# ConvGLU up projection: GpSimd takes the low part of the value half's weights, and the later convolutions accumulate in a PSUM bank

## The chip, the cores and the metric

The kernel runs on one core of a Trainium2 chip, in one launch. Its time is the device time of an execution in microseconds (us). The engines are named as the profile names them: PE (TensorE matmul), PEld (its weight load), DVE (VectorE), ACT (ScalarE), POOL (GpSimd) and SP (SyncE, which issues most DMAs).

## What is computed

One layer of a hybrid backbone: a token mixer, then a ConvGLU channel mixer, on 512 tokens (8 rows of 64) of width 1024. The change is in the channel mixer, whose reference is:

```python
def _conv_ffn(h, rows, w_up, conv_w, conv_b, w_down):      # w_up (1024, 2 x 2816), w_down (2816, 1024)
    a, val = _split(h @ w_up, (D_FF, D_FF))
    img = a.reshape(bsz, rows, length // rows, D_FF)
    a = lax.conv_general_dilated(img, conv_w[:, :, None, :], (1, 1), 'SAME', ...,
                                 feature_group_count=D_FF) + conv_b      # 3 x 3, each channel by itself
    return (jax.nn.gelu(a.reshape(bsz, length, D_FF), approximate=False) * val) @ w_down
```

## The kernel before

**Products.** All operands are fp32. A matrix is split into a high part rounded to fp32r and a low part, the rest; a product is then three matmuls per piece (high x high, high x low, low x high). The up projection goes through the 2816 channels in 22 steps `f` of 128 channels. A step has two products, one for the image half (the columns that are convolved) and one for the value half. A product is 24 matmuls (8 pieces of the inner dimension, 3 each) into one PSUM bank of the pool `pm` (four banks, tiles `mm`). Below, product j = 2f is the image half of step f, and j = 2f + 1 its value half; there are 44. The other four banks are the pool `pg` (tiles `gl`), which the up projection leaves alone and the down projection uses as accumulators.

**Weights.** For each product a tile `raw` (128 x 1024, 512 KB) is loaded by SP (L148) into one of four buffers; ACT rounds it into `wh` (L138), and DVE subtracts, `wl = raw - wh` (L139). `wh` and `wl` have five buffers each, so ACT can round a tile as soon as PE has ended the product five before it.

**A step's elementwise work** is `conv_part(f, pa, pv)`. ACT copies the image bank `pa` into the SBUF tile `ca` (L1422) and writes bias plus centre tap into the SBUF tile `cacc` (L1424). DVE adds the eight other taps, each a scalar_tensor_tensor `cacc = ca * w + cacc` (L1430). ACT applies Gelu (L1431), DVE multiplies by the value bank `pv` (L1432). After each odd step DVE forms four sums over token halves (L1413 to L1416), which a Strassen-like down projection needs.

**Down projection.** It needs the gated channels as its left operand and `ffn_w_down` as weights. Weight tiles come into the same four `raw` buffers (L1457) and, with an addition on the way, into `b22` tiles (load by SP, L1453; accumulating DMA by POOL, L1454). DVE adds two halves of a `raw` tile (L1485), forms `t2` (L1489) and the low parts (L1475, L354); ACT rounds (L1474, L353). PE accumulates (L1532) in eight banks: four `gl` (the products `p1` and `p5`, two each) and four `mm` (`p7`, `p6`).

**Order.** Each engine works off its own queue in order. A scheduler places the instructions of the traced program in these queues, so code written in one place can stand among that of the next step, and preparation of the down projection stands among the last steps of the up projection.

Of the kernel before, what the change touches and what calls it, by code (L numbers as in the profile page):

```python
# [8 lines left out]
F32 = mybir.dt.float32  # L9
# [3 lines left out]
AF = mybir.ActivationFunctionType  # L13
ALU = mybir.AluOpType
AX = mybir.AxisListType

P = 128
# [3 lines left out]
KT = 8  # L21
NH = 4
FF = 2816
FT = 22
GW = 64
# [8 lines left out]
def backbone_kernel(  # L34
# [7 lines left out]
    V, A, G, T = nc.vector, nc.scalar, nc.gpsimd, nc.tensor  # L42
# [11 lines left out]
    def nm(s):  # L54
        cnt[0] += 1
        return f"{s}_{cnt[0]}"

    def heap(shape, dt=F32, s="h"):
        return hp.tile(shape, dt, tag="h", name=nm(s))

    def late(shape, dt=F32, s="l"):
        return lp.tile(shape, dt, tag="l", name=nm(s))
# [4 lines left out]
    def mm():  # L67
        return pm.tile([P, 512], F32, tag="mm", name=nm("mm"))

    def gl():  # L70
        return pg.tile([P, 512], F32, tag="gl", name=nm("gl"))

    def const(shape, s, dt=F32):
        return cp.tile(shape, dt, tag=s, name=s)
# [57 lines left out]
    def raw_tile(kn, n):  # L132
        return wp.tile([P, kn, n], F32, tag="raw", name=nm("raw"), bufs=4)

    def split_new(raw, kn, n):
        wh = wp.tile([P, kn, n], F32R, tag="wh", name=nm("wh"))
        wl = wp.tile([P, kn, n], F32R, tag="wl", name=nm("wl"))
        A.copy(wh, raw)  # L138
        V.tensor_tensor(wl, raw, wh.bitcast(F32), op=ALU.subtract)  # L139
        return wh, wl  # L140

    def w_cols(w, c0, n=P, k0=0, kn=KT, scaled=False):
        ap = w[k0 * P:(k0 + kn) * P, c0:c0 + n].rearrange("(k p) c -> p k c", p=P)
        held = []

        def load():
            held.append(raw_tile(kn, n))
            dma(held[0], ap)  # L148

        def split():  # L150
            if not scaled:
                return split_new(held.pop(), kn, n)
            raw = held.pop()
            wh = wp.tile([P, kn, n], F32R, tag="wh", name=nm("wh"))
            wl = wp.tile([P, kn, n], F32R, tag="wl", name=nm("wl"))
            for kk in range(kn):
                g_ = gng[:, k0 + kk:k0 + kk + 1]
                A.mul(wh[:, kk, :], raw[:, kk, :], g_)
                V.scalar_tensor_tensor(wl[:, kk, :], raw[:, kk, :], g_, wh[:, kk, :].bitcast(F32), op0=ALU.mult,
                                       op1=ALU.subtract)  # L160
            return wh, wl

        loads.append((len(specs), load))
        specs.append(split)

    def w_wide(w, scaled=False):
        for hf in range(2):
            for k in range(KT // 2):
                w_cols(w, hf * 512, 512, 2 * k, 2, scaled)

    def w_strassen(w, c0):
# [32 lines left out]
        def split_raw(name, j):  # L204
            return lambda: split_new(raws.pop((name, j)), 2, 512)
# [12 lines left out]
        def split_b11(j):  # L218
            def split():
                raws["b11k", j] = raws["b11", j]  # L220
                return split_new(raws.pop(("b11", j)), 2, 512)
            return split
# [11 lines left out]
    for h in range(1, NH):  # L234
        if h > 1:
            w_cols(wi, O_V + h * 256, 256, 0, 4)
            w_cols(wi, O_V + h * 256, 256, 4, 4)
        for hh in ((1, 2), (3,), ())[h - 1]:
            w_cols(wi, O_K + hh * P)
            w_cols(wi, O_Q + hh * P)  # L240
# [10 lines left out]
    w_wide(w_o[0])  # L251
    for f in range(FT):
        w_cols(ffn_w_up[0], f * P)
        w_cols(ffn_w_up[0], FF + f * P)

    splits = {}
    pos = [0, 0, 0]
# [13 lines left out]
    def weights(lead=1, ahead=AHEAD):  # L271
        i = pos[2]
        pos[2] += 1
        stream_split(i + 1 + lead)
        stream_load(i + 1 + ahead)
        return splits.pop(i)
# [50 lines left out]
    for d in range(2):  # L327
        raw = late([96, 512], s="w2r")
# [393 lines left out]
    for k in range(KT):  # L722
# [10 lines left out]
        n = 0  # L733
# [286 lines left out]
    for t in range(2):  # L1020
        ps = mm()
        for k in range(KT):
            wh, wl = fv[k // 2][1:]
# [128 lines left out]
    ccol = const([P, 220], "ccol")  # L1152
# [24 lines left out]
    for j in range(KT):  # L1177
        w = weights()
# [225 lines left out]
    gact, s12, s4 = [], [], []  # L1404
    flat = lambda z: z.rearrange("p r w -> p (r w)")

    def token_sums(p):

        e, o = flat(gact[2 * p]), flat(gact[2 * p + 1])
        s = late([P, 2, 256], s="s12")  # L1410
        if p % 2 == 0:
            s4.append(late([P, 2, 256], s="s4"))
        V.tensor_tensor(s[:, 0, :], o[:, 256:], e[:, 256:], op=ALU.subtract)  # L1413
        V.tensor_tensor(s[:, 1, :], s[:, 0, :], e[:, :256], op=ALU.add)
        V.tensor_tensor(e[:, 256:], e[:, :256], e[:, 256:], op=ALU.subtract)
        V.tensor_tensor(s4[-1][:, p % 2, :], s[:, 1, :], o[:, :256], op=ALU.subtract)  # L1416
        s12.append(s)

    def conv_part(f, pa, pv):
        wcol = lambda tap: ccol[:, tap * FT + f:tap * FT + f + 1]  # L1420
        a_ = heap([P, 8, GW], s="ca")
        A.copy(a_, pa)  # L1422
        acc = heap([P, 8, GW], s="cacc")
        A.activation(acc, pa, AF.Identity, bias=ccol[:, 198 + f:199 + f], scale=wcol(4))  # L1424
        for tap in (0, 1, 2, 3, 5, 6, 7, 8):
            dy, dx = tap // 3 - 1, tap % 3 - 1
            r0, r1 = max(0, -dy), 8 - max(0, dy)
            c0, c1 = max(0, -dx), GW - max(0, dx)
            o = acc[:, r0:r1, c0:c1]
            V.scalar_tensor_tensor(o, a_[:, r0 + dy:r1 + dy, c0 + dx:c1 + dx], wcol(tap), o, op0=ALU.mult, op1=ALU.add)  # L1430
        A.activation(acc, acc, AF.Gelu)  # L1431
        V.tensor_tensor(acc, acc, pv.rearrange("p (r w) -> p r w", w=GW), op=ALU.mult)  # L1432
        gact.append(acc)
        if f % 2:
            token_sums(f // 2)

# [3 lines left out]
    for i in range(4):  # L1440
        prod_cm(pss[i][:, 256:], ws[i], h2, 256, 256)
    conv_part(0, pss[0], pss[1])
    conv_part(1, pss[2], pss[3])

    NP = FT // 2
# [106 lines left out]
    for f in range(2, FT):  # L1552
        pa = mm()
        prod_cm(pa, weights(), h2)
        pv = mm()
        prod_cm(pv, weights(), h2)
        if f == FT - 2:
            d_load(4)
        if f == FT - 1:
            d_load(7)  # L1560
            for i in range(LEAD):
                prep(i)
        conv_part(f, pa, pv)
# [163 lines left out]
```

## Time and profile before

| | |
|---|---|
| time, median of 3 runs | 930.37 us |
| the profiled execution | 931.34 us, of which the span of the trace is 929.6 us |
| PE busy | 907.7 us, 98% of the span |
| DVE busy | 755.2 us, 81% |
| ACT busy | 447.8 us, 48% |
| POOL busy | 52.8 us, 6% |

The span is the time from the first to the last instruction of the trace; 1.74 us of the execution lie around it. The trace gives for each instruction its engine, its line in the code and its start; for idle time it names what ended it.

### The profile page before, as it was taken

Reading aid. Unit: us, or ns where it says so; the run is one execution under the profiler, and the core shown is the slowest. Engines: PE = TensorE matmul, PEld = TensorE weight load, DVE = VectorE, ACT = ScalarE, POOL = GpSimd, SP = SyncE. Lnnn points to the kernel's source line nnn. Section 1 sums busy time; section 2 is a strip of 40 time slices with the busy share of each in tenths; the row PEclk is TensorE's granted clock in tenths of the full one; section 3 lists DMA queues with packets and bytes.
Section 4 is the critical chain, followed back from the end, with each engine's and each line's share of the span. In section 5 each row is a group of like instructions: output and inputs, shape, how many; then the busy total and the mean of one; then the engine's idle time right before and its main releaser. Section 6 shows DMA issues by size and latency. Waiting matters only on the chain.

```text
span 929.6 us, 12825 instructions
## 1 busy us (share of the span) xinstructions
PE 907.7 (98%) x4695; PEld 761.1 (82%) x4695; DVE 755.2 (81%) x1349; ACT 447.8 (48%) x787; POOL 52.8 (6%) x80
## 2 busy tenths in 40 slices
PE   6999999999999999999999999999999999999996
PEld 5776898988878888888878888988888888878885
DVE  5567758689689978866789987798888888999797
ACT  5136546457443337755652334543333333366574
POOL 3000000000000011112100000000000000132000
PEclk9999999999999999999999999999999999999998
DMA  9940411132077384885649642333333333399432
GB/s 275 336 130 24 136 47 46 46 96 64 23 228 231 112 227 90 230 212 144 187 127 340 228 142 78 102 94 95 109 92 91 93 109 110 85 251 246 127 101 91
DMA packets 123547, 130.06 MB, mean 140 GB/s; under 512 B 6953, under 2 KB 84085, under 8 KB 123485
## 3 DMA queue, kind: packets, MB, share of 16 engines
q1 hardware_dynamic: 114781, 115.75, 40.2%
q0 software_dynamic: 6976, 12.28, 8.0%
q10 hardware_dynamic: 1728, 1.22, 0.4%
q8 instruction: 37, 0.61, 0.3%
q14 instruction: 25, 0.20, 0.1%
HBM read 127.13 MB, written 2.10 MB: 139 GB/s over the span
## 4 chain that ended last, share of the span: by engine, by line
PE 82%; DVE 10%; ACT 2%; DMA 2%; issue 2%; SPq 1%; ACTq 0%; DVEq 0%
PE mm L361 27%; PE mm L387 13%; PE gl L434 7%; PE gl L1532 6%; PE mm L434 5%; PE mm L1532 4%; PE gl L387 4%; PE gl L876 3%; PE mm L380 3%; DVE cacc L1430 2%; PE mm L372 1%; PE mm L666 1%; PE mm L980 1%; DVE bc L844 1%; DVE wl L139 1%
## 5 line engine op out<-in xcount | busy, mean ns | idle before, releaser
L138 ACT CAST wh<-raw 128x1024 fp32r<-128x1024 f32 x110 | 115.4, 1052 | 148.8 <-PE mm L361 99.8
L139 DVE TENSOR_TENSOR wl<-raw,wh 128x1024 fp32r<-128x1024 f32 x110 | 133.9, 1220 | 43.7 <-ACT wh L138 43.3
L361 PE MATMUL mm<-h2h,wh 128*128 128x512 f32 (+1 forms) x352 | 133.5, 379 | 0.0
L361 PE MATMUL mm<-h2l,wh 128*128 128x512 f32 (+1 forms) x352 | 133.5, 379 | 0.0
L361 PE MATMUL mm<-h2h,wl 128*128 128x512 f32 (+1 forms) x352 | 133.5, 379 | 0.0
L1430 DVE SCALAR_TENSOR_TENSOR cacc<-ca,ccol,cacc 128x441 f32<-128x441 f32 (+2 forms) x176 | 121.7, 695 | 4.1
L361 PEld LDWEIGHTS mm<-h2h,wh 128*128 128x128 f32 x352 | 66.2, 188 | 12.5
L361 PEld LDWEIGHTS mm<-h2l,wh 128*128 128x128 f32 x352 | 66.2, 188 | 12.4
L361 PEld LDWEIGHTS mm<-h2h,wl 128*128 128x128 f32 x352 | 66.2, 188 | 12.4
L1125 DVE SCALAR_TENSOR_TENSOR acc<-wa,cs,acc 128x512 f32<-128x512 f32 x64 | 45.1, 744 | 2.1 <-DMA wa<-in_w_ada_dram 2.1
L387 PE MATMUL mm<-wh,trh 128*128 128x512 f32 x112 | 44.4, 397 | 0.0
L387 PE MATMUL mm<-wh,trl 128*128 128x512 f32 x112 | 44.0, 392 | 0.0
L387 PE MATMUL mm<-wl,trh 128*128 128x512 f32 x112 | 43.7, 390 | 0.0
L1431 ACT ACTIVATE cacc<-cacc 128x512 f32<-128x512 f32 x22 | 13.9, 633 | 58.5 <-DVE cacc L1430 58.5
L361 PE MATMUL mm<-hxh,wh 128*128 128x512 f32 x104 | 41.7, 401 | 0.0
L361 PE MATMUL mm<-hxh,wl 128*128 128x512 f32 x104 | 41.0, 394 | 0.0
L361 PE MATMUL mm<-hxl,wh 128*128 128x512 f32 x104 | 40.7, 391 | 0.0
L1474 ACT CAST wh<-raw 128x1024 fp32r<-128x1024 f32 x22 | 23.0, 1052 | 20.5 <-PE mm L1532 6.1
L1454 POOL DMA_DIRECT2D b<-in_ffn_w_down_dram x11 | 9.4, 878 | 370.5 <-DMA b<-in_ffn_w_down_dram 356.8
L1475 DVE TENSOR_TENSOR wl<-raw,wh 128x1024 fp32r<-128x1024 f32 x22 | 26.8, 1219 | 4.4 <-ACT wh L1474 4.3
L186 POOL DMA_DIRECT2D tt<-in_w_in_dram x24 | 20.9, 1135 | 166.2 <-DVE hu L1207 77.5
L434 PE MATMUL mm<-wh,hxh 128*128 128x512 f32 x72 | 28.0, 389 | 0.0
(489 smaller groups left out, 2323.5 us busy)
## 6 DMA issues: line engine op xcount, KB each, us to landing
raw<-in_w_in_dram SPq DMA_DIRECT2D x54, 512.0 KB
wa<-in_w_ada_dram SPq DMA_DIRECT2D x96, 256.0 KB
raw<-in_ffn_w_up_dram SPq DMA_DIRECT2D x44, 512.0 KB
raw<-in_ffn_w_down_dram SPq DMA_DIRECT2D x22, 512.0 KB
tt<-in_w_in_dram POOLq DMA_DIRECT2D x24, 256.0 KB, 7.7
raw<-in_w_br_a_dram SPq DMA_DIRECT2D x8, 512.0 KB
raw<-in_w_br_b_dram SPq DMA_DIRECT2D x8, 512.0 KB
raw<-in_w_o_dram SPq DMA_DIRECT2D x8, 512.0 KB
```

Of the source, the lines that this page charges most:

```text
L138: A.copy(wh, raw)
L139: V.tensor_tensor(wl, raw, wh.bitcast(F32), op=ALU.subtract)
L361: T.matmul(ps, a[:, k, :], b[:, c0:c0 + n], start=(k == 0 and i == 0), stop=(k == KT - 1 and i == 2))
L380: T.matmul(ps, a[:, t * P:(t + 1) * P], b[:, k % 4, :], start=(k == 0 and i == 0), stop=(k == KT - 1 and i == 2))
L387: T.matmul(ps, a, b[:, k % 2, :], start=(k == 0 and i == 0), stop=(k == KT - 1 and i == 2))
L434: T.matmul(ps[t], a, b[:, kk, :], start=(first and i == 0), stop=(j == 1 and kk == 1 and i == 2), skip_group_check=again)
L876: T.matmul(ps, p_, q_, start=(start and z == 0), stop=(stop and z == 2))
L1125: V.scalar_tensor_tensor(acc[j], w_, cs[:, k, 0:1], acc[j], op0=ALU.mult, op1=ALU.add)
L1430: V.scalar_tensor_tensor(o, a_[:, r0 + dy:r1 + dy, c0 + dx:c1 + dx], wcol(tap), o, op0=ALU.mult, op1=ALU.add)
L1474: A.copy(wh, raw)
L1475: V.tensor_tensor(wl, raw, wh.bitcast(F32), op=ALU.subtract)
L1532: T.matmul(ps, a[:, t * P:(t + 1) * P], w[b][:, j, c0:c0 + n], start=(first and i == 0), stop=(last and i == 2), skip_group_check=again)
```

## The change

For steps f >= 3 the subtraction that makes `wl` of the value half is issued on GpSimd instead of VectorE. For steps f >= 11 the convolution's accumulator is a `gl` PSUM bank: ACT writes bias and centre tap there, DVE accumulates the taps there, and Gelu reads it and writes the SBUF tile `cacc`, which the rest of the kernel uses as before. Lines below L1423 are one higher than before in the changed kernel.

```diff
-    def split_new(raw, kn, n):
+    def split_new(raw, kn, n, eng=None):
         ...
         A.copy(wh, raw)
-        V.tensor_tensor(wl, raw, wh.bitcast(F32), op=ALU.subtract)
+        (eng or V).tensor_tensor(wl, raw, wh.bitcast(F32), op=ALU.subtract)
         return wh, wl
...
     for f in range(FT):
         w_cols(ffn_w_up[0], f * P)
-        w_cols(ffn_w_up[0], FF + f * P)
+        w_cols(ffn_w_up[0], FF + f * P, eng=G if f >= 3 else None)
...
         A.copy(a_, pa)
-        acc = heap([P, 8, GW], s="cacc")
-        A.activation(acc, pa, AF.Identity, bias=ccol[:, 198 + f:199 + f], scale=wcol(4))
+        g_ = heap([P, 8, GW], s="cacc")
+        acc = gl().rearrange("p (r w) -> p r w", w=GW) if f >= FT // 2 else g_
+        A.activation(acc, pa.rearrange("p (r w) -> p r w", w=GW), AF.Identity, bias=..., scale=wcol(4))
         for tap in (0, 1, 2, 3, 5, 6, 7, 8):
             ...
             V.scalar_tensor_tensor(o, a_[...], wcol(tap), o, op0=ALU.mult, op1=ALU.add)
-        A.activation(acc, acc, AF.Gelu)
-        V.tensor_tensor(acc, acc, pv.rearrange("p (r w) -> p r w", w=GW), op=ALU.mult)
-        gact.append(acc)
+        A.activation(g_, acc, AF.Gelu)
+        V.tensor_tensor(g_, g_, pv.rearrange("p (r w) -> p r w", w=GW), op=ALU.mult)
+        gact.append(g_)
```

The change also moves instructions at three places. On PE, at the start of the down projection, `gl_7770` to `gl_7773` are the four accumulators before; the rows are the fifth to the twelfth matmul of the down projection.

```order
L1532 MATMUL gl_7771<-wl_7716,eh_7720 128x512
L1532 MATMUL gl_7771<-wh_7715,el_7721 128x512
L1532 MATMUL gl_7772<-wh_7715,sh_7724 128x512
L1532 MATMUL gl_7772<-wl_7716,sh_7724 128x512
L1532 MATMUL gl_7772<-wh_7715,sl_7725 128x512
L1532 MATMUL gl_7773<-wh_7715,sh_7724 128x512
L1532 MATMUL gl_7773<-wl_7716,sh_7724 128x512
L1532 MATMUL gl_7773<-wh_7715,sl_7725 128x512
```

In the changed kernel `gl_7781` to `gl_7784` are these accumulators, and `mm_7787` one of the others. The rows are the thirty-fourth to the forty-first matmul of the down projection.

```order
L1533 MATMUL mm_7787<-wh_7807,sh_7754 128x512
L1533 MATMUL mm_7787<-wl_7808,sh_7754 128x512
L1533 MATMUL mm_7787<-wh_7807,sl_7755 128x512
L1533 MATMUL gl_7784<-wh_7725,sh_7734 128x512
L1533 MATMUL gl_7784<-wl_7726,sh_7734 128x512
L1533 MATMUL gl_7784<-wh_7725,sl_7735 128x512
L1533 MATMUL gl_7784<-wh_7745,sh_7754 128x512
L1533 MATMUL gl_7784<-wl_7746,sh_7754 128x512
```

The fourth `gl` accumulator begins as the tenth matmul before, and as the thirty-seventh now; its bank is the one in which step 21 accumulates its convolution.

On POOL, at the end of the up projection, the queue now reads as follows (the last three subtractions, of products 39, 41 and 43, and the first accumulating DMAs of the down projection).

```order
L139 TENSOR_TENSOR wl_7498<-raw_7424,wh_7497 128x1024
L139 TENSOR_TENSOR wl_7580<-raw_7501,wh_7579 128x1024
L139 TENSOR_TENSOR wl_7665<-raw_7583,wh_7664 128x1024
L1455 DMA b_1450_7640<-in_ffn_w_down_dram 128x512
L1455 DMA b_1452_7645<-in_ffn_w_down_dram 128x512
L1455 DMA b_1461_7719<-in_ffn_w_down_dram 128x512
```

Before, the queue held the DMAs alone; all 19 subtractions now stand ahead of them.

On DVE, around the convolution of step 18, this stood before (`raw_7634` and `raw_7707` are the second and third weight tile of the down projection; `wl_7571`, `wl_7602` and `wl_7655` belong to products 41, 42 and 43).

```order
L139 TENSOR_TENSOR wl_7571<-raw_7493,wh_7570 128x1024
L1430 SCALAR_TENSOR_TENSOR cacc_7476<-ca_7474,ccol,cacc_7476 128x7x63
L1430 SCALAR_TENSOR_TENSOR cacc_7476<-ca_7474,ccol,cacc_7476 128x448
L1430 SCALAR_TENSOR_TENSOR cacc_7476<-ca_7474,ccol,cacc_7476 128x7x63
L1430 SCALAR_TENSOR_TENSOR cacc_7476<-ca_7474,ccol,cacc_7476 128x8x63 x2
L1485 TENSOR_TENSOR raw_7634<-raw_7634 128x512
L1430 SCALAR_TENSOR_TENSOR cacc_7476<-ca_7474,ccol,cacc_7476 128x7x63
L139 TENSOR_TENSOR wl_7602<-raw_7524,wh_7601 128x1024
L1430 SCALAR_TENSOR_TENSOR cacc_7476<-ca_7474,ccol,cacc_7476 128x448
L1430 SCALAR_TENSOR_TENSOR cacc_7476<-ca_7474,ccol,cacc_7476 128x7x63
L1432 TENSOR_TENSOR cacc_7476<-cacc_7476,mm_7443 128x512
L1485 TENSOR_TENSOR raw_7707<-raw_7707 128x512
```

The same stretch now (`raw_7643` and `raw_7717` are the second and third weight tile, `wl_7611` belongs to product 42):

```order
L1431 SCALAR_TENSOR_TENSOR gl_7484<-ca_7481,ccol,gl_7484 128x7x63
L1431 SCALAR_TENSOR_TENSOR gl_7484<-ca_7481,ccol,gl_7484 128x448
L1431 SCALAR_TENSOR_TENSOR gl_7484<-ca_7481,ccol,gl_7484 128x7x63
L1431 SCALAR_TENSOR_TENSOR gl_7484<-ca_7481,ccol,gl_7484 128x8x63 x2
L1486 TENSOR_TENSOR raw_7643<-raw_7643 128x512
L1431 SCALAR_TENSOR_TENSOR gl_7484<-ca_7481,ccol,gl_7484 128x7x63
L139 TENSOR_TENSOR wl_7611<-raw_7532,wh_7610 128x1024
L1431 SCALAR_TENSOR_TENSOR gl_7484<-ca_7481,ccol,gl_7484 128x448
L1431 SCALAR_TENSOR_TENSOR gl_7484<-ca_7481,ccol,gl_7484 128x7x63
L1433 TENSOR_TENSOR cacc_7483<-cacc_7483,mm_7450 128x512
L1486 TENSOR_TENSOR raw_7717<-raw_7717 128x512
```

The subtractions of products 41 and 43 have left DVE's queue; the additions on the weight tiles have kept their places among the taps. The second weight tile is loaded into the buffer of product 41's `raw`, and the fourth into that of product 43's: both are free when POOL has subtracted, where before DVE freed them.

More of the change, by code (lines that the diff above doesn't have):

```diff
@@ L138, in split_new, with w_cols @@
         A.copy(wh, raw)
-        V.tensor_tensor(wl, raw, wh.bitcast(F32), op=ALU.subtract)
+        (eng or V).tensor_tensor(wl, raw, wh.bitcast(F32), op=ALU.subtract)
         return wh, wl
-    def w_cols(w, c0, n=P, k0=0, kn=KT, scaled=False):
+    def w_cols(w, c0, n=P, k0=0, kn=KT, scaled=False, eng=None):
         ap = w[k0 * P:(k0 + kn) * P, c0:c0 + n].rearrange("(k p) c -> p k c", p=P)
@@ L151, in split @@
             if not scaled:
-                return split_new(held.pop(), kn, n)
+                return split_new(held.pop(), kn, n, eng)
             raw = held.pop()
@@ L1422, in conv_part @@
         A.copy(a_, pa)
-        acc = heap([P, 8, GW], s="cacc")
-        A.activation(acc, pa, AF.Identity, bias=ccol[:, 198 + f:199 + f], scale=wcol(4))
+        g_ = heap([P, 8, GW], s="cacc")
+        acc = gl().rearrange("p (r w) -> p r w", w=GW) if f >= FT // 2 else g_
+        A.activation(acc, pa.rearrange("p (r w) -> p r w", w=GW), AF.Identity, bias=ccol[:, 198 + f:199 + f], scale=wcol(4))
         for tap in (0, 1, 2, 3, 5, 6, 7, 8):
```

## The prediction

> **What bounds the kernel now.** I read the busy shares first, then the up projection in stretches of four steps, then what PE waited for.
>
> ```profile
> span 929.6 us, 12825 instructions
> PE 907.7 (98%) x4695; PEld 761.1 (82%) x4695; DVE 755.2 (81%) x1349; ACT 447.8 (48%) x787; POOL 52.8 (6%) x80
> core 0: us, PE busy (x) PEld busy (x) DVE busy (x) ACT busy (x) POOL busy (x), PEclk, DMA share, GB/s
> 684.73:728.25 43.52, 43.52 (x193) 36.05 (x192) 36.67 (x53) 15.61 (x21) 0.00 (x0) 1.00 0.33 97
> 728.25:771.77 43.52, 43.52 (x193) 36.05 (x192) 36.68 (x53) 15.62 (x21) 0.00 (x0) 1.00 0.34 97
> 771.77:815.29 43.52, 43.52 (x193) 36.05 (x192) 39.54 (x60) 17.79 (x27) 3.78 (x5) 1.00 0.39 104
> engine line waited for: us in total, times, longest us
> PE mm L1532 <- DVE cacc L1432: 0.8, 1, 0.8
> ```
>
> The reader is to see that PE is busy in the whole of each stretch, at full clock, while DVE has a sixth of it free. The last two lines are all of PE's waits from 575 to 921 us: one, of 0.8 us, behind the up projection. Around it PE's queue reads:
>
> ```profile
> 815.06 0.39 PE L361 MATMUL mm<-h2h,wl 128*128 128x512 f32 x1
> 815.29 0.39 PE L1532 MATMUL gl<-wh,eh 128*128 128x512 f32 x1
> 825.72 0.39 PE L1532 MATMUL gl<-wl,eh 128*128 128x512 f32 x1
> 826.90 0.47 PE L1532 MATMUL mm<-wh,sh 128*128 128x512 f32 x1 [0.80 <-DVE cacc L1432]
> ```
>
> From the first to the forty-seventh matmul of the down projection are 46 intervals in 10.43 us, 0.2267 us each. A product of 24 takes 5.44 us, a step 10.88. Product j ends at 815.29 - 5.44 x (43 - j): product 36 at 777.2, 38 at 788.1, 41 at 804.4. After 825.72 the next matmul was due at 825.95 and began at 826.90: **0.95 us** is all that a faster elementwise path can give. The subtractions and taps that the change touches are not on PE's path before 815.
>
> **The change, part by part.** *DVE's load.* These are the two groups touched, and two events of a step:
>
> ```profile
> L139 DVE TENSOR_TENSOR wl<-raw,wh 128x1024 fp32r<-128x1024 f32 x110 | 133.9, 1220 | 43.7 <-ACT wh L138 43.3
> L1430 DVE SCALAR_TENSOR_TENSOR cacc<-ca,ccol,cacc 128x441 f32<-128x441 f32 (+2 forms) x176 | 121.7, 695 | 4.1
> 690.14 1.06 ACT L138 CAST wh<-raw 128x1024 fp32r<-128x1024 f32 x1 [1.08 <-PE mm L361]
> 700.01 0.69 DVE L1432 TENSOR_TENSOR cacc<-cacc,mm 128x512 f32<-128x512 f32 x1 [0.76 <-ACT cacc L1431]
> ```
>
> DVE loses 19 x 1.22 = 23.2 us. Its busy time falls from 36.68 / 4 = 9.17 us a step to 7.95, of 10.88. PE doesn't wait for it, so this is worth nothing by itself. What hides it: the image product of that step ended at 690.1, when ACT's rounding was released, so the value product ended at 695.5; its bank is needed again by the value product two steps on, 16.3 us later at 711.9, and DVE let go of it at 700.7. **DVE may fall 11.2 us behind before PE waits.**
>
> *POOL's subtraction.* The trace has none, so I bound its duration t. Below stands DVE's 1.22 us for the same tile. Above, POOL's own rows:
>
> ```profile
> L1116 POOL MEMSET acc<- 128x512 f32 x8 | 5.0, 1107 | 198.6 <-PE gl L876 198.6
> L779 POOL MEMSET pmask<- 128x512 f32 x2 | 1.0, 538 | 37.0 <-PE gl L590 37.0
> L1713 POOL MEMSET const-float32-0.0<- 128x1 f32 x1 | 0.1, 99 | 0.3 <-issue 0.3
> ```
>
> Writing 512 elements costs 0.538 - 0.099 = 0.44 us over the start, 0.88 us for 1024. The subtraction has two reads and a write: 0.10 + 2 x 0.88 = 1.9 us if the write is covered, 0.10 + 3 x 0.88 = 2.7 if nothing is; I take the middle, **t = 2.3 us**. By the slow memset it would be 3 x 2 x 1.107 = 6.6, the upper end. The Trainium skill, "GPSIMD Engine Reference", section "Elementwise — side-by-side cycle accounting", gives 4497 ns for a tensor_tensor of 2048 elements; my estimate from that page is 2.25 us for 1024, and the sum would be the same. No run here shows it yet.
>
> For the products t is hidden. `wh` of product 41 is begun as product 36 ends, so PE needs the pair four products later: 4 x 5.44 - 1.06 = 20.7 us. POOL's queue has one subtraction per 10.88 us, and no DMA stands between two of them.
>
> *Accumulating in PSUM.* The trace has DVE adding in place in a PSUM bank, beside SBUF:
>
> ```profile
> 876.16 0.69 DVE L1654 TENSOR_TENSOR gl<-gl,u 128x512 f32<-128x512 f32 x1
> 877.35 0.68 DVE L1655 TENSOR_TENSOR p7s<-gl,p7s 128x512 f32<-128x512 f32 x1
> 780.12 3.67 DVE L1430 SCALAR_TENSOR_TENSOR cacc<-ca,ccol,cacc 128x441 f32<-128x441 f32 x5
> 825.47 0.69 DVE L1489 TENSOR_TENSOR t<-raw,b 128x512 f32<-128x512 f32 x1
> 826.08 0.68 DVE L1432 TENSOR_TENSOR cacc<-cacc,mm 128x512 f32<-128x512 f32 x1
> ```
>
> Duration is the same within 0.01 us. Five taps of one chain take 3.67, one every 0.73 us, against 0.61 for independent neighbours. How long a dependent tap waits for a PSUM result isn't shown: I take no change, bounded by 0.12 us either way. For ACT's write and Gelu's read I also take no change, within 0.2 us each.
>
> *The hand-over is where it counts.* Before, PE's forty-eighth matmul waited for L1432 of step 21, the last reader of an `mm` bank. Now the fourth `gl` accumulator, at the thirty-seventh matmul (815.29 + 36 x 0.2267 = **823.45**), needs the bank in which step 21 is convolved, so it waits for that step's Gelu. And the additions on the second and fourth weight tile, in the midst of steps 18 and 19, wait for loads that POOL's subtraction releases. I follow DVE through steps 18 to 21, with durations from the timeline and, for the load, from the chain that ended last:
>
> ```profile
> 777.18 1.06 ACT L138 CAST wh<-raw 128x1024 fp32r<-128x1024 f32 x1 [1.08 <-PE mm L361]
> 778.14 0.58 ACT L1422 COPY ca<-mm 128x512 f32<-128x512 f32 x1
> 778.61 0.78 ACT L1424 ACTIVATE cacc<-mm,ccol 128x512 f32<-128x512 f32 x1
> 780.23 3.57 DMA raw<-in_ffn_w_down_dram
> 783.83 0.69 DVE L1485 TENSOR_TENSOR raw<-raw 128x512 f32<-128x512 f32 x1
> 800.30 0.42 DVE L1413 TENSOR_TENSOR s<-cacc,cacc 128x256 f32<-128x256 f32 x1
> 801.78 1.22 DVE L1475 TENSOR_TENSOR wl<-raw,wh 128x1024 fp32r<-128x1024 f32 x1
> 821.95 1.22 DVE L1475 TENSOR_TENSOR wl<-raw,wh 128x1024 fp32r<-128x1024 f32 x1
> 823.08 0.68 DVE L1430 SCALAR_TENSOR_TENSOR cacc<-ca,ccol,cacc 128x448 f32<-128x448 f32 x1
> 825.05 0.63 ACT L1431 ACTIVATE cacc<-cacc 128x512 f32<-128x512 f32 x1 [0.78 <-DVE cacc L1430]
> ```
>
> From these rows: a weight tile lands 3.6 us after its release; the four sums take 1.5 us, a large subtraction 1.13, other independent operations 0.6, Gelu 0.65, the multiplication 0.7.
> - Step 18: taps from 779.4; five end at 783.05. `wh` of product 41 ends at 778.25, POOL at 780.55, and the second tile lands at 784.15: a wait of 1.1 us. Addition, tap, subtraction, two taps: 788.0. Gelu and multiplication: 789.4. The third tile, released by that subtraction at 786.55, lands at 790.2; addition until 790.8.
> - Step 19: ACT, behind Gelu (788.7), rounds product 43 until 789.75 and has the accumulator ready at 791.0. Five taps: 794.7. The fourth tile: 789.75 + 2.3 + 3.6 = 795.65, a wait of 0.95. The rest as above: 800.8, with the sums 802.3, with a subtraction 803.4.
> - Step 20: eight taps and two small subtractions among them: 810.3; Gelu and multiplication 811.7; seven operations of down-projection preparation: 815.9.
> - Step 21: four taps with other work between them (2.45), that work (2.95), four taps in a chain (2.9): 824.2. Gelu until 824.9.
>
> PE waits from 823.45 to 824.9, **1.45 us, where it waited 0.95**. Behind it the other accumulators and left operands come in time, the closest (`sl` of the third weight tile, at 829.25 for PE's 829.4) with 0.2 us to spare. From there DVE's work per pair of channel tiles is 9.5 us for PE's 10.9, as the order of these operations is what it was, so nothing is given back.
>
> Sum: 931.34 + 1.45 - 0.95 = 931.8 for an execution like the profiled one, which lies 0.97 above the median; **930.9 us**.
>
> **What t does.** Both loads shift with t, so beyond 2.3 us each further 1 us costs 2. At t = 1.2 both waits go, Gelu ends at 823.3 and PE's wait vanishes: 929.4. At 6.6 it is 930.9 + 2 x 4.3 = 939.5.
>
> **The rivals.**
> - *The hand-over closes*: t below 1.6 or a PSUM chain quicker by 0.12 x 24 taps = 2.9 us. For it: DVE has 3 subtractions less in those steps. Against: ACT hands it the accumulators at 791.0 whatever it does. 930.37 - 0.95 = 929.4 us.
> - *Slower, the late loads*: POOL needs over 3.3 us, so that the second and fourth weight tile of the down projection come late and step 21's Gelu with them. From 3.3 us on the cost is 2.5 us and more: 933 to 939.5. For it: the slow memset row. Against: the quick one.
> - *The PSUM accumulator is not as quick as SBUF*: 0.12 us on each of the 24 chained taps of steps 18 to 21 is 2.9 us, 933.8 us. For it: that dependent taps already cost 0.12 us more than independent ones. Against: the equal durations of L1654 and L1655.
> - *DVE is shut out while POOL reads*. In steps 3 to 10 the taps read two SBUF tiles, as POOL does. If DVE stood still during each subtraction, a step would cost it 7.95 + t = 10.25 us of 10.88 at 2.3, which hides; it falls behind from t = 2.93, and PE waits once 8 x (t - 2.93) exceeds 11.2, at t = 4.3. At 6.6 that is 29.4 - 11.2 = 18.2 us on top of the late loads: 958. No row shows POOL reading SBUF beside DVE's taps, and the price needs a t near the upper end, so I give it little. The Trainium skill, "SBUF — State Buffer", section "Who interferes with whom", says that a DVE instruction with two SBUF inputs and a GpSimd instruction that reads SBUF exclude each other for a whole instruction. By that rule this rival's condition holds, and the PSUM accumulator of steps 11 on takes the taps out of it; the price still hangs on t.
>
> **How the numbers follow.** Forecast (929.9 to 932.5): 0.5. Hand-over closes: 0.25. Late loads: 0.15. Slow PSUM taps: 0.07. Shut out with large t: 0.03. The range runs from the floor, 929.4 less 0.2 for the spread of runs, to 936 (t = 4.8, more than twice the quick memset's pace); what lies above I give 0.08. Within 2%, or 18.6 us, which is about what a measurement of this kernel can tell from no change, lie all cases but the last at t over 5.7: faster 0.01, same 0.96, slower 0.03.
>
> **What would show it.** Right: PE without waits to 815, one POOL row of about 2.3 us x19, DVE's L1486 waiting for a load in steps 18 and 19, and the wait of the hand-over at a `gl` bank for ACT's Gelu, near 1.5 us. Wrong: any PE wait for `wl` or an `mm` bank before 815, a POOL row over 4 us, taps longer than 0.75 us in steps 3 to 10 (shut out) or 11 to 21 (PSUM), or PE's interval no longer 0.2267 us, which I have taken as fixed.

## Result: 1.0% slower, lost behind the up projection

The changed kernel takes **940.0 us** in the median of 4 runs (939.0 to 940.55), the kernel before 930.37 us (a run of it at 1010.39 us is left out): a ratio of 1.0102, 95% interval 1.0082 to 1.0122. The forecast was 930.9 us, the range 929.2 to 936.0; the time lies above it. The profiled execution took 939.0 us, 7.66 us more than that of before, and its span is 7.7 us longer; the medians differ by 9.6 us, as the profiled execution of before lay above its median and this one below. The first lines of the changed kernel's page:

```profile
span 937.3 us, 12843 instructions
PE 909.7 (97%) x4695; PEld 762.0 (81%) x4695; DVE 761.2 (81%) x1330; ACT 442.6 (47%) x787; POOL 98.7 (11%) x99
```

All of PE's waits from 570 to 930 us (us in total, times, longest):

```profile
PE gl L1533 <- ACT eh L353: 4.1, 1, 4.1
PE gl L1533 <- ACT cacc L1432: 2.7, 1, 2.7
```

Two things stand out. DVE has 19 subtractions less and is busy for 761.2 us, where it was 755.2. And PE's one wait of 0.8 us has become two, of 4.1 and 2.7 us. Around them PE's queue (start, duration, instruction) reads:

```profile
814.20 0.39 PE L361 MATMUL mm<-h2h,wl 128*128 128x512 f32 x1
818.67 0.80 PE L1533 MATMUL gl<-wh,eh 128*128 128x512 f32 x1 [4.08 <-ACT eh L353]
828.95 0.39 PE L1533 MATMUL mm<-wh,sl 128*128 128x512 f32 x1
831.99 0.50 PE L1533 MATMUL gl<-wh,sh 128*128 128x512 f32 x1 [2.65 <-ACT cacc L1432]
```

The first row is the last matmul of the up projection. It ends its turn at 814.20 + 0.23 = 814.43, 0.86 us earlier than before (815.29): up to there PE lost nothing. Then it idles 4.24 us until 818.67. Between 818.67 and the 37th matmul, due at 828.95 + 0.23 = 829.18, lie 36 matmuls in 10.51 us; at 0.2267 us each they would take 8.16. The third part of the loss is in these 2.35 us, and the granted clock (the column of 0.50 and 1.00) shows where:

```profile
816.75:823.00 6.25, 4.33 (x10) 3.34 (x11) 5.53 (x10) 5.03 (x9) 0.00 (x0) 0.50 0.17 50
823.50:829.00 5.50, 5.50 (x26) 4.50 (x24) 5.50 (x9) 1.54 (x2) 1.58 (x3) 1.00 0.73 203
```

PE's clock was halved while it idled and stayed so until 823. Then comes the second wait, 829.18 to 831.99, 2.81 us. The sum: 4.24 + 2.35 + 2.81 = 9.40, less the 0.95 of before and the 0.86 of the earlier start, is 7.6 of the 7.7 us.

### The profile page after: what moved, and what is told of

It reads as the page before. It is cut to its first block, busy times and chain, and to the rows that moved or that the text cites. A ratio compares the mean times of both kernels' runs of the same rounds, so it can differ in the third digit from the quotient of the medians.

```text
span 937.3 us, 12843 instructions
## 1 busy us (share of the span) xinstructions
PE 909.7 (97%) x4695; PEld 762.0 (81%) x4695; DVE 761.2 (81%) x1330; ACT 442.6 (47%) x787; POOL 98.7 (11%) x99
## 4 chain that ended last, share of the span: by engine, by line
PE 77%; DVE 16%; ACT 3%; issue 2%; DMA 1%; ACTq 0%; DVEq 0%
PE mm L361 20%; PE mm L387 13%; PE gl L434 7%; PE gl L1533 6%; DVE gl L1431 6%; PE mm L434 5%; PE mm L1533 4%; PE gl L387 4%; PE gl L876 3%; PE mm L380 3%; DVE wl L139 1%; PE mm L666 1%; PE mm L372 1%; DVE s L1414 1%; PE mm L980 1%
## 5 line engine op out<-in xcount | busy, mean ns | idle before, releaser
L139 DVE TENSOR_TENSOR wl<-raw,wh 128x1024 fp32r<-128x1024 f32 x91 | 110.8, 1221 | 34.6 <-ACT wh L138 34.2
L139 POOL TENSOR_TENSOR wl<-raw,wh 128x1024 fp32r<-128x1024 f32 x19 | 45.8, 2412 | 309.0 <-ACT wh L138 296.0
L1431 DVE SCALAR_TENSOR_TENSOR cacc<-ca,ccol,cacc 128x441 f32<-128x441 f32 (+2 forms) x88 | 69.3, 791 | 7.8 <-ACT cacc L1425 5.7
L1431 DVE SCALAR_TENSOR_TENSOR gl<-ca,ccol,gl 128x441 f32<-128x441 f32 (+2 forms) x88 | 61.5, 698 | 7.7 <-ACT gl L1425 5.5
L1432 ACT ACTIVATE cacc<-gl 128x512 f32<-128x512 f32 x11 | 6.6, 598 | 74.6 <-DVE gl L1431 74.6
L1432 ACT ACTIVATE cacc<-cacc 128x512 f32<-128x512 f32 x11 | 7.0, 633 | 72.3 <-DVE cacc L1431 72.3
```

What stands on the lines that cost most here:

```text
L139: (eng or V).tensor_tensor(wl, raw, wh.bitcast(F32), op=ALU.subtract)
```

## Where the lag comes from

Both waits are for the elementwise chain of steps 20 and 21, which is late. POOL's group (busy us, then mean ns of one):

```profile
L139 POOL TENSOR_TENSOR wl<-raw,wh 128x1024 fp32r<-128x1024 f32 x19 | 45.8, 2412 | 309.0 <-ACT wh L138 296.0 <-PE mm L361 13.0
```

DVE's groups from 586 to 840 us, shapes apart:

```profile
L1414 DVE TENSOR_TENSOR s<-s,cacc 128x256 f32<-128x256 f32 x11 | 21.4, 1943 | 0.3
L1431 DVE SCALAR_TENSOR_TENSOR cacc<-ca,ccol,cacc 128x441 f32<-128x441 f32 x44 | 36.0, 822 | 6.5 <-ACT cacc L1425 5.7
L1431 DVE SCALAR_TENSOR_TENSOR gl<-ca,ccol,gl 128x441 f32<-128x441 f32 x44 | 29.9, 680 | 6.6 <-ACT gl L1425 5.5
```

POOL's subtraction takes 2.41 us, where 2.3 was forecast. But the sum L1414, an addition of two SBUF tiles, takes 1.94 us in the mean, and the taps in SBUF 0.82, where the same taps into PSUM take 0.68. The kernel before has for them:

```profile
L1414 DVE TENSOR_TENSOR s<-s,cacc 128x256 f32<-128x256 f32 x11 | 4.7, 424 | 0.3
L1430 DVE SCALAR_TENSOR_TENSOR cacc<-ca,ccol,cacc 128x441 f32<-128x441 f32 x88 | 59.3, 676 | 1.6
```

The timeline at the end of step 11 shows it in one instance, ACT, POOL and DVE together:

```profile
717.38 0.60 ACT L1432 ACTIVATE cacc<-gl 128x512 f32<-128x512 f32 x1 [6.02 <-DVE gl L1431]
717.87 1.05 ACT L138 CAST wh<-raw 128x1024 fp32r<-128x1024 f32 x1
718.73 0.42 DVE L1413 TENSOR_TENSOR s<-cacc,cacc 128x256 f32<-128x256 f32 x1
718.81 0.59 ACT L1422 COPY ca<-mm 128x512 f32<-128x512 f32 x1
719.00 2.42 POOL L139 TENSOR_TENSOR wl<-raw,wh 128x1024 fp32r<-128x1024 f32 x1 [7.25 <-ACT wh L138]
719.19 2.51 DVE L1414 TENSOR_TENSOR s<-s,cacc 128x256 f32<-128x256 f32 x1
722.30 0.67 DVE L1431 SCALAR_TENSOR_TENSOR gl<-ca,ccol,gl 128x441 f32<-128x441 f32 x1
```

L1414 begins 0.19 us after POOL and ends 0.28 us after it: it stood still for 2.1 us. The first tap of step 12 begins at 722.30, although its operands were ready at 720.05 (719.28 + 0.77, the centre tap). The encounter is no accident. POOL's subtraction follows ACT's rounding, that follows Gelu in ACT's queue, and Gelu is what DVE has just worked for: so POOL starts while DVE has its sums before it (behind the Gelu of an odd step) or the next step's first taps (behind that of an even one).

The Trainium skill, "SBUF — State Buffer", section "Who interferes with whom", has the rule: a DVE instruction with two SBUF inputs and a GpSimd instruction that reads SBUF exclude each other for a whole instruction. The rows agree, with 2.1 us lost at a sum; among the taps it is 1.1 us, as seven of them take 6.19 us at 642.55 and 5.09 at 632.87.

What follows is a loop: DVE's taps of step f, then on ACT, in its queue's order, Gelu of f, a rounding, `ca` and the centre tap of f + 1, then DVE's taps of f + 1. A delay of DVE goes once round and comes back as a later `ca`. The lag of `ca` against the kernel before is therefore the quantity to follow. Starts of `ca`, in us (executions without a lag differ by up to 1.3 us in where step 3 falls):

| kernel | step 3 | step 11 | step 12 | step 18 | step 21 |
|---|---|---|---|---|---|
| before | 614.94 | 701.98 | 712.87 | 778.14 | 813.43 |
| changed | 618.61 | 709.17 | 718.81 | 783.32 | 821.20 |
| GpSimd part alone | 619.09 | 709.63 | 720.41 | 788.36 | 825.83 |
| memsets on GpSimd | 614.87 | 701.51 | 712.40 | 777.67 | 812.22 |
| Gelu a step later | 619.80 | 710.36 | 713.39 | 778.47 | 812.19 |

In the changed kernel the lag is 3.7 us at step 3, 7.2 at step 11, 5.2 at step 18 and 7.8 at step 21. What is there at step 3 comes from the first two subtractions: at 595.18 and 603.38 they fall among taps, and seven taps take 6.85 us and six 6.28, where the kernel with memsets (below) has 4.72 and 4.50. Behind step 18 the addition on a weight tile, whose two inputs are both in SBUF, meets POOL's last subtraction (796.42 to 798.82) and takes 2.52 us instead of 0.69; the chain that ended last runs through it:

```profile
796.85 2.52 DVE L1486 TENSOR_TENSOR raw<-raw 128x512 f32<-128x512 f32 x1 [0.72 <-DMA raw<-in_ffn_w_down_dram]
```

Yet DVE's busy time between steps 5 and 11 is nearly the same. The window of before:

```profile
641.26:707.69 66.43, 66.43 (x295) 55.03 (x294) 56.09 (x80) 24.39 (x31) 0.00 (x0) 1.00 0.33 95
```

And that of the changed kernel:

```profile
641.26:707.69 66.43, 66.43 (x295) 55.01 (x294) 56.95 (x71) 20.54 (x29) 14.47 (x6) 1.00 0.32 92
```

That is nine instructions fewer and 0.9 us more busy time, with some 10 us idle in both: DVE did not run out of time, the time was lost where the loop passes.

## Experiments

Theory A is this exclusion with the loop. Theory B: the scheduler's new order on ACT (Gelu of step 2 ahead of `ca` of step 3) makes the lag. Theory C: the PSUM accumulators at the hand-over make the loss. The diffs are against the changed kernel.

**GpSimd writes without reading.**

```diff
-        (eng or V).tensor_tensor(wl, raw, wh.bitcast(F32), op=ALU.subtract)
+        if eng is None: V.tensor_tensor(wl, raw, wh.bitcast(F32), op=ALU.subtract)
+        else:
+            for k0 in range(0, kn, kn // 2):
+                eng.memset(wl[:, k0:k0 + kn // 2, :].bitcast(F32), 0.0)
```

> The 19 subtractions on GpSimd become 19 pairs of memsets of half a tile, which read no SBUF; the low part of the value half's weights is thus left out for f >= 3. Orders on ACT and PE are as in the changed kernel. Theory A (the GpSimd subtraction shuts out a DVE operation with two SBUF inputs, and the loop DVE - ACT - DVE carries the lag): s<-s,cacc falls from 1943 ns to some 424, the lag of `ca` against PE doesn't grow from step to step, 929.5 to 932. Theory B (the order on ACT, Gelu ahead of the next image copy, makes the lag): lag and both waits of PE stay, 937 to 940. Theory C (the PSUM accumulators at the hand-over): 937 to 940 as well.

931.66 us, ratio 1.0005 (0.9997 to 1.0014). POOL's group:

```profile
L143 POOL MEMSET wl<- 128x512 f32 x38 | 18.9, 528 | 327.6 <-PE mm L365 327.6
```

DVE's sum:

```profile
L1418 DVE TENSOR_TENSOR s<-s,cacc 128x256 f32<-128x256 f32 x11 | 4.7, 424 | 0.3
```

PE's only wait:

```profile
PE gl L1537 <- ACT cacc L1436: 1.5, 1, 1.5
```

No stretch, no lag (table), one wait of 1.5 us at the `gl` bank. The orders are those of the changed kernel, so B falls, and so does C. The memsets are also shorter (2 x 0.53 us for 2.41), but they do meet the sums: one pair runs from 646.41 to 647.40, and the four sums beside it, from 645.84 to 647.39, take 0.42 to 0.43 us each. So it is not GpSimd being at work that holds DVE up; a memset as long as the subtraction was not run.

**Each half of the change alone.**

```diff
-        acc = gl().rearrange("p (r w) -> p r w", w=GW) if f >= FT // 2 else g_     # GpSimd part alone
+        acc = gl().rearrange("p (r w) -> p r w", w=GW) if f >= FT else g_
```
```diff
-        w_cols(ffn_w_up[0], FF + f * P, eng=G if f >= 3 else None)                 # PSUM part alone
+        w_cols(ffn_w_up[0], FF + f * P, eng=None)
```

> GpSimd subtracts for f >= 3, but all convolutions accumulate in SBUF. Theory A: from step 11 on the taps have two SBUF inputs too and are shut out in even steps, so the lag goes on growing by some 0.9 us per two steps; step 21's multiplication ends later than the 831 us of the changed kernel, 938 to 945, with PE waiting for an `mm` bank instead of a `gl` bank. Theory B: as the changed kernel, less what the gl bank costs, 936 to 940. Theory C: back to 930 to 932.

> DVE does all subtractions; the convolutions accumulate in a PSUM bank from f = 11 on. Theories A and B (the order on ACT is that of before): no lag, 930 to 932, with at most a wait of some 1 to 2 us at a `gl` bank. Theory C: 937 to 940.

The GpSimd part alone: **946.09 us**, ratio 1.0164 (1.015 to 1.0178). The PSUM part alone: 931.17 us, 1.0003 (0.9994 to 1.0012). PE's waits in the former:

```profile
PE mm L1533 <- DVE cacc L1433: 4.3, 1, 4.3
PE gl L1533 <- ACT eh L353: 3.8, 1, 3.8
PE mm L361 <- DVE cacc L1433: 3.0, 3, 1.7
```

And the only one in the latter:

```profile
PE gl L1533 <- ACT cacc L1432: 1.5, 1, 1.5
```

GpSimd makes the loss, and the PSUM accumulators take more than a third of it back: from step 11 on the taps are no longer shut out (680 ns). Without them the lag grows to 10.2 us at step 18, and there PE begins to wait in the up projection itself (third line). The time lies 1 us above the expected 938 to 945: these three waits were not in it.

**GpSimd from step 11 on only.**

```diff
-        w_cols(ffn_w_up[0], FF + f * P, eng=G if f >= 3 else None)
+        w_cols(ffn_w_up[0], FF + f * P, eng=G if f >= 11 else None)
```

> GpSimd subtracts only for f >= 11, where the taps accumulate in PSUM; the order on ACT is that of before. Theory A: the taps can't be shut out, only the sum s<-s,cacc of the odd steps (some 2 us, six times), which the odd steps' own idle time takes back: no lag at step 11, under 2 us at step 21; 929.5 to 933. Theory B: 930 to 932. Theory C: 937 to 940.

933.53 us, ratio 1.0038 (1.0025 to 1.0051), 0.5 us above the expected range. PE's wait:

```profile
PE gl L1533 <- ACT cacc L1432: 2.6, 1, 2.6
```

One of the sums, partly stretched:

```profile
L1416 DVE TENSOR_TENSOR s<-s,cacc 128x256 f32<-128x256 f32 x11 | 9.0, 817 | 0.0
```

The encounters of the sums remain (it is now L1415 and L1416 that are hit most), but they don't add up: the lag is 1.1 us at step 11 and 0.2 at step 18. At step 21 it is 2.2, because POOL's last subtraction meets the addition L1486 here too, which the expectation had left out:

```profile
791.37 2.38 DVE L1486 TENSOR_TENSOR raw<-raw 128x512 f32<-128x512 f32 x1 [0.85 <-DMA raw<-in_ffn_w_down_dram]
```

**The same delay on DVE, with no GpSimd read.** The kernel with memsets, and:

```diff
+        if f >= 3 and f % 2 == 0:                                      # ahead of the taps
+            for _ in range(2): V.tensor_scalar(acc, acc, 1.0, None, op0=ALU.mult)
...
+        if f >= 3 and f % 2:                                           # ahead of the sums
+            for _ in range(4): V.tensor_scalar(g_, g_, 1.0, None, op0=ALU.mult)
```

> As the run with memsets (nothing shut out, low part of the value half's weights left out for f >= 3), but DVE itself is given the delay, from f = 3 on: four multiplications by 1 ahead of the sums of an odd step (some 1.6 to 2 us), two ahead of the taps of an even step (some 1 to 1.4 us). DVE's busy time is then some 9.5 us of a step's 10.88. Theory A (the loop DVE - ACT - DVE carries a delay whatever makes it): `ca` slips by some 0.3 to 1 us per two steps although DVE still idles, and PE waits at the hand-over as in the changed kernel, 933 to 940. Rival (the step by which the prediction priced it: what fits into DVE's idle time is hidden; only GpSimd's exclusion costs): no lag, 930 to 932.

936.38 us, ratio 1.0057 (1.0045 to 1.0069). PE's wait:

```profile
PE gl L1543 <- ACT cacc L1439: 4.4, 1, 4.4
```

The operations added ahead of the sums:

```profile
L1443 DVE TENSOR_SCALAR cacc<-cacc 128x512 f32<-128x512 f32 x40 | 17.6, 441 | 1.1
```

The same window as above:

```profile
641.26:707.69 66.43, 66.43 (x295) 55.01 (x294) 55.74 (x90) 23.44 (x31) 5.93 (x12) 1.00 0.33 95
```

DVE is busy for 55.74 us, less than the 56.09 of before, which had no lag, and `ca` slips by some 0.4 us per two steps: it is at 705.15 in step 11 (before: 701.98). So the loop carries a delay of any origin, and a DVE share of 84% says nothing of it. This shows the step by which I priced the exclusion to be wrong, apart from the exclusion itself. From step 11 on the lag falls again, from 3.2 us to 1.0 at step 18, though nothing is shut out here: so the end of the exclusion need not be all that the PSUM accumulators bring. What else they do is not shown.

**The loop opened.**

```diff
+        while pending: pending.pop()()                    # behind the centre tap of this step
...
-        A.activation(g_, acc, AF.Gelu)
-        ...                                               # multiplication, sums
+        def finish():
+            A.activation(g_, acc, AF.Gelu)
+            ...
+        if f < 2 or f == FT - 1: finish()
+        else: pending.append(finish)
```

> The changed kernel with Gelu, multiplication and sums of step f (f >= 2) written behind image copy and centre tap of step f + 1; on ACT this moves Gelu behind `ca` and the centre tap from step 11 on, before that the queue is as it was. Theory A: from step 11 on the loop is open (the next step's taps no longer wait for this step's Gelu), the lag of about 5 us at step 11 is worked off, 930 to 934, although GpSimd still subtracts. Rival (DVE as a whole has too little time when it is shut out 2 us a step): 936 to 940.

930.94 us, ratio 1.0 (0.9992 to 1.0009). `ca` of steps 11 and 12 in ACT's timeline:

```profile
710.36 0.57 ACT L1422 COPY ca<-mm 128x512 f32<-128x512 f32 x1
713.39 0.59 ACT L1422 COPY ca<-mm 128x512 f32<-128x512 f32 x1
```

PE's waits:

```profile
PE gl L1541 <- ACT eh L353: 0.4, 1, 0.4
PE gl L1541 <- ACT cacc L1435: 0.3, 1, 0.3
```

The sum that is still held up:

```profile
L1414 DVE TENSOR_TENSOR s<-s,cacc 128x256 f32<-128x256 f32 x11 | 13.0, 1181 | 0.1
```

This is the whole change, all 19 subtractions on GpSimd included. At step 11 `ca` is as late as in the changed kernel; with Gelu behind it in ACT's queue, the next `ca` follows after 3.03 us, and from there on keeps PE's pace of 10.88. The exclusion goes on (1.18 us for 0.42) and costs nothing.

**All convolutions in PSUM,** then with GpSimd at odd f only, then with odd f up to 17:

```diff
-        acc = gl().rearrange("p (r w) -> p r w", w=GW) if f >= FT // 2 else g_
+        acc = gl().rearrange("p (r w) -> p r w", w=GW) if f >= 0 else g_
-        w_cols(ffn_w_up[0], FF + f * P, eng=G if f >= 3 else None)      # second and third kernel
+        w_cols(ffn_w_up[0], FF + f * P, eng=G if f >= 3 and f % 2 else None)         # second
+        w_cols(ffn_w_up[0], FF + f * P, eng=G if 3 <= f < 18 and f % 2 else None)    # third
```

> All 22 convolutions accumulate in a PSUM bank; GpSimd subtracts for f >= 3 as in the changed kernel. Theory A: no tap is stretched in any step, only the sum s<-s,cacc of the odd steps (2.5 us); two steps then take no longer than PE's 21.8 us, as in the second half of the changed kernel, so that the lag doesn't grow: 931 to 935. Rival (a DVE operation on PSUM is held up as well, or the lag has another source): 938 or more.

> As the run before, with GpSimd subtracting only for odd f >= 3: these ten subtractions follow the Gelu of an even step and fall among taps that accumulate in PSUM; those of even f, which fall on the sums, are DVE's. Theory A: nothing is stretched, 929.5 to 931.5 with a wait at the `gl` bank of about 1.5 us. Rival (each GpSimd subtraction costs DVE time wherever it falls): half of the loss of the run before.

> All 22 convolutions in PSUM, GpSimd subtracting for odd f from 3 to 17 only, so that no load of the down projection waits for GpSimd. In the run with odd f up to 21, the fourth weight tile's load lay behind GpSimd's subtraction and DVE waited 3.4 us for it. If that load made its loss, PE's only wait is the 1.5 us of the run without GpSimd, 930 to 932; if GpSimd beside PSUM taps costs by itself, 932.5 to 934 again.

933.81 us (ratio 1.0029, 1.002 to 1.0038), 933.48 (1.0024, 1.0015 to 1.0033) and 931.54 (1.0006, 0.9997 to 1.0015). PE's only wait in the first:

```profile
PE gl L1533 <- ACT cacc L1432: 2.6, 1, 2.6
```

In the second:

```profile
PE gl L1533 <- ACT cacc L1432: 3.1, 1, 3.1
```

In the third:

```profile
PE gl L1533 <- ACT cacc L1432: 1.3, 1, 1.3
```

In the first, no lag is left at step 18 (`ca` at 777.18); behind it one L1486 waits 1.98 us for its load and the next takes 2.50 us beside POOL. In the second nothing is stretched, and yet my expectation of 929.5 to 931.5 was missed. The profiled execution, the slowest of its twelve (931.17 to 936.12), shows where. Its chain that ended last, near step 19:

```profile
790.12 2.61 POOL wl L139
792.75 5.40 DMA raw<-in_ffn_w_down_dram
```

And its DVE timeline:

```profile
798.24 0.69 DVE L1486 TENSOR_TENSOR raw<-raw 128x512 f32<-128x512 f32 x1 [3.38 <-DMA raw<-in_ffn_w_down_dram]
```

The fourth weight tile of the down projection, released by POOL's last subtraction, took 5.40 us to land, and DVE stood 3.38 us. Why this load took 5.40 us is open. With GpSimd out of it from f = 18 on, this wait and the loss are gone (third kernel). So GpSimd beside PSUM taps costs nothing by itself that the runs can tell, while its last two subtractions, ahead of the late loads, cost 2 us.

**Is it the bank at the hand-over?**

```diff
-        acc = gl().rearrange("p (r w) -> p r w", w=GW) if f >= FT // 2 else g_
+        acc = gl().rearrange("p (r w) -> p r w", w=GW) if FT // 2 <= f < 18 else g_
```

> The changed kernel, but the last four convolutions accumulate in SBUF again, so that no `gl` bank is held when the down projection begins; PE's order there is that of before. Theory A: the lag at step 18 is that of the changed kernel (`ca` near 783.3 us), and it is paid at the fourth accumulator or at an `mm` bank instead: 936 to 941. Theory C (the `gl` bank held by step 21's convolution is what costs): 930 to 934.

942.43 us, ratio 1.0121 (1.0105 to 1.0136); `ca` of step 18 at 783.94. PE's waits:

```profile
PE mm L1533 <- DVE cacc L1433: 4.8, 1, 4.8
PE gl L1533 <- ACT eh L353: 3.1, 1, 3.1
```

With no `gl` bank held the same lag is paid at an `mm` bank, and more of it (1.4 us above the expected range): C falls a second time.

**Shorter subtractions.**

```diff
-        (eng or V).tensor_tensor(wl, raw, wh.bitcast(F32), op=ALU.subtract)
+        if eng is None: V.tensor_tensor(wl, raw, wh.bitcast(F32), op=ALU.subtract)
+        else:
+            for k0 in range(0, kn, kn // 4):
+                z = slice(k0, k0 + kn // 4)
+                eng.tensor_tensor(wl[:, z, :], raw[:, z, :], wh[:, z, :].bitcast(F32), op=ALU.subtract)
```

> The changed kernel with each GpSimd subtraction cut into four of 128x256 (some 0.6 to 0.7 us each). If the exclusion lasts one instruction, a DVE operation of two SBUF inputs is held up by at most one quarter: no DVE row of the up projection over some 1.3 us, s<-s,cacc some 0.8 to 1.1 us in the mean, GpSimd held up in turn, and by theory A a smaller lag: 931 to 937. If GpSimd keeps the port from one instruction to the next, or if it gets it back each time ahead of DVE, the delay per subtraction stays about 2 us: 938 to 941.

938.46 us, ratio 1.0081 (1.0067 to 1.0094). The sums of step 11 in the timeline:

```profile
717.28 3.40 POOL L144 TENSOR_TENSOR wl<-raw,wh 128x256 fp32r<-128x256 f32 x4 [6.81 <-ACT wh L138]
717.48 0.85 DVE L1419 TENSOR_TENSOR s<-s,cacc 128x256 f32<-128x256 f32 x1
718.25 0.96 DVE L1420 TENSOR_TENSOR cacc<-cacc 128x256 f32<-128x256 f32 x1
719.13 0.96 DVE L1421 TENSOR_TENSOR s<-s,cacc 128x256 f32<-128x256 f32 x1
```

The two engines now take turns: three sums of 0.42 take 0.85 to 0.96 us, and four quarters 3.40 us instead of 2.4. So the exclusion lasts one instruction, as expected. The second half of that expectation, a smaller lag and 931 to 937 us, failed, and the time lies in the range of its rival (938 to 941): three sums lose some 1.5 us together instead of 2.1, and the time falls by less than 2 us.

**The widest margin.** All subtractions on DVE, PSUM from f = 11, and Gelu a step later as above:

> No subtraction on GpSimd, PSUM accumulators from f = 11 on, and Gelu, multiplication and sums of a step behind the next step's image copy and centre tap: the version with the most room for DVE at the hand-over. PE's waits behind the up projection under 0.8 us in all, where before had 0.95: 929.5 to 931, not to be told from before. Slower than 932 if a Gelu that comes a step later makes the left operands late.

931.08 us, ratio 1.0003 (0.9995 to 1.0012), 0.1 us above the expected range. PE's only wait there:

```profile
PE gl L1541 <- ACT cacc L1435: 0.3, 1, 0.3
```

The wait at the hand-over is down from 0.95 to about 0.3 us, and the time isn't to be told from before. No version found beats the kernel before; what was left there was under 1 us.

## Why the prediction was wrong, by its steps

- *Right:* PE has no wait before the up projection ends; POOL's subtraction takes 2.41 us for my 2.3; a PSUM tap takes as long as one in SBUF (680 and 676 ns), chain and all. The bank in which step 21 is convolved does make PE wait for Gelu: forecast 1.45 us, measured 1.5 us with the PSUM part alone, whose 931.17 us agrees with the 930.9 forecast. The bank and the wait are as forecast for that half of the change. That the size agrees is partly luck: my path to 1.45 us had 2.05 us of waits for loads behind POOL, and three subtractions fewer on DVE, and this run has neither.
- *Wrong, the price of the exclusion.* The rival "DVE is shut out while POOL reads" had the mechanism, and beside it the rule of the Trainium skill by which its condition holds, and I gave it 0.03. I priced it by busy time, 7.95 + 2.3 = 10.25 us of a step's 10.88, "which hides", and let it decide only from 2.93 us on. But DVE and ACT wait for one another within a step, so some of DVE's idle time is not to be had: in steps 4 and 5 of the changed kernel it stood 0.76 us for each Gelu and 1.41 us for a centre tap. I also counted only the taps; the sums of the odd steps and L1486 have two SBUF inputs as well, and PSUM doesn't take them out. In the runs: two steps took 22.6 us in the first half of the changed kernel (`ca` from 641.26 in step 5 to 663.89 in step 7) for PE's 21.76, with DVE busy 86%; and a delay of like size made by DVE's own operations made `ca` slip likewise, by 0.4 us per two steps for the 0.9 here. My own sign of this rival, taps over 0.75 us, was met (0.82).
- *Wrong, the tolerance.* "DVE may fall 11.2 us behind before PE waits" held: PE first waited in the up projection in the run where the lag passed 10 us. But I took a lag below it as free. At the hand-over the tolerance ends, because PE's next operand is the elementwise result itself; all of the lag but the slack there is paid.
- *Wrong, the starting point.* I followed steps 18 to 21 from taps at 779.4 us, the state of before. `ca` of step 18 came 5.2 us later.
- *Not seen:* the first matmul of the down projection waits for `eh`, which stands behind Gelu of step 20 on ACT (4.24 us of the 7.6), and the halved clock after it (2.35 us).
- *Wrong for the changed kernel, the late loads.* The additions on the second and fourth weight tile, which I had waiting 1.1 and 0.95 us, don't wait there (790.99 and 802.87): DVE comes to them late itself. With less lag such waits show, though not at the price I gave: in one kernel DVE stood 3.38 us, with POOL at 2.6 us and the load at 5.40 instead of 3.57.

## What to carry to other kernels

An engine that is busy 85% of a step need not have 15% free if it sits in a loop with another engine's queue: follow one iteration through both queues in order, and see whether a delay comes back to its start later or is absorbed. A lag that the buffers tolerate during a stage is paid where the next stage uses the result itself, so follow it to the hand-over. Before work goes to GpSimd, list which DVE operations have two SBUF inputs at the moment at which it will start; here a queue order that lets the lag drain took the whole loss away, PSUM operands in all steps most of it (933.81 us), and PSUM operands with GpSimd at odd f up to 17 only all of it (931.54).

## What the runs showed of the hardware beside this

- PE's granted clock fell to 0.50 after an idle stretch, for 3 us and more, and an idle stretch of 2.6 us was enough in one run and not in another. Behind the 2.6 us wait of the run with all convolutions in PSUM:

```profile
826.50:829.50 3.00, 3.00 (x8) 2.34 (x7) 3.00 (x8) 1.94 (x4) 0.00 (x0) 0.50 0.19 35
```

  Behind the 2.6 us wait of the run with GpSimd from step 11 on:

```profile
827.00:830.00 3.00, 3.00 (x15) 2.45 (x14) 3.00 (x8) 2.19 (x4) 0.00 (x0) 1.00 0.49 95
```

  Eight matmuls in 3 us there, fifteen here. In the changed kernel the low clock lasted for over 6 us, 816.75 to 823. The Trainium skill, "TensorE: Matmul & The Clock Gate", Part 1, gives half rate after an idle window of about 3.4 us that runs freely; the low stretches of some 3 and 6 us fit one such window and two, but an idle stretch of 2.6 us should then not have sufficed. So a wait of PE of 2.6 us cost more than its length in one run and not in the other, and that of 4.24 us in the changed kernel 2.35 us more.
- GpSimd's exclusion is mutual and lasts one instruction (0.85 to 0.96 us for sums of 0.42 beside quarters; POOL's four quarters 3.40 us), and a memset of GpSimd, which only writes, held up nothing.
